# FFN layer one: inner sums in place over a column pair, and the weight difference T1 made during layer one's first half

## The chip, the cores and the metric

The kernel runs on one core of a Trainium2 chip. The metric is the device time of one execution in microseconds. TensorE (PE) multiplies 128-row tiles into PSUM, VectorE (DVE) and ScalarE (ACT) work on tiles in SBUF and PSUM, GpSimd (POOL) does little here, and SyncE (SP) issues nearly all DMAs from one queue, in order. Each engine executes its own instructions in the order in which they were written out for it; they wait for each other through semaphores.

## The reference

One decoder block over 2048 tokens of width 1024, in float32. The part before the FFN (a combined input projection, a pooling mixer, a stick-breaking attention, an output projection) is not touched by the change. The FFN that follows is:

```python
hn2 = rmsnorm(h, norm2_g)
up = jnp.einsum('bsd,df->bsf', hn2, w_up)        # 1024 -> 4096
act = jnp.square(jax.nn.relu(up))
h = h + jnp.einsum('bsf,fd->bsd', act, w_down)   # 4096 -> 1024
return rmsnorm(h, final_g)
```

## The kernel before, in words

**Arithmetic.** Each float32 operand is split into two rounded parts, hi and lo (`split`: ScalarE copies hi at L146, VectorE subtracts to get lo at L147), and each product is three matmuls: hi by hi, hi by lo, lo by hi. Both FFN layers use a scheme with seven block products instead of eight for a 2 x 2 block product (Winograd's form). It needs sums and differences of the blocks of both operands. For the activations these are called A11, A12, A22, S1, S2, S3, S4; the products are P1 to P7.

**Layer one** (`up`, matmuls at L1054). The 2048 tokens make two pairs of 512-token blocks, `q` = 0 and 1, done one after the other; these are layer one's two halves. In each, 16 columns `m` of the hidden dimension are walked in the order 0, 8, 1, 9, and so on (list `cols`): m and m + 8 are the two columns of a pair. A column has seven slots of 12 matmuls, in the order P2, P6, P5, P7, P1 of the next column, P4, P3. After each slot `post` takes what is finished out of PSUM: after P6 and P7 copies `u2`, `u3` of a bank that then goes on being summed into (L987), after P2, P7, P4 and P3 an activation block (relu L981, square L982), and the sums for layer two (L1014 to L1027), stored to DRAM tensors `sd` (L976). All these temporaries come from one pool of 13 buffers of 128 x 512 (`avp`). Weights for a slot are loaded (`rb`, L905, 1 MB a column), summed (L909 to L912) and split (`hw`) four slots ahead of their matmuls. During the first half the second pair's own sums are made too, in the columns m = 2 to 5 (`sums_second`, L940 to L946).

**Inner sums.** Three of layer two's seven products (P4, P5, P2, with the operands A22, S1, A12) are themselves done by seven inner products. Their activations need sums over the column pair and both token pairs. Before the change, in the second half, `inner_sums` does nothing at the first column of a pair but keep the block. At the second column (m from 8 on) two row blocks of the first token pair, loaded by `inner_rows` (L870) after P1, P2 and P7, meet the two blocks of the second; four VectorE operations (L881, L883, L885, L887) make four sums, two of them in fresh buffers `j1`, `j2`, and each is stored to `sdi` (L879).

**Layer two** (`down`, matmuls at L1392 for whole products, L1221 for inner ones). The order is P1, P6, P7 (eight steps each), then P4, P5, P2 (28 inner steps each), then P3. A step of P1, P6 or P7 takes one block of weights (512 KB, `wr`) and two blocks of rows (`ar`, 512 KB each), splits them into `wd` and `ad`, and runs 48 matmuls. `make_ahead` keeps up to three steps made ahead; the first one is issued at high priority, during layer one's end.

**Weight sums of layer two.** T1 = B12 - B11 and T2 = B21 - (B22 - T1) are differences of blocks of `w_down`. Before the change `more_weights`, called in every step of P1, loads B12, subtracts the step's B11 (L1115), stores T1 to DRAM (`td`, L1122) and makes four inner differences of each pair of T1 blocks, in place (`inner_weights`, L1106, stored to `wi` at L1107). In P6 the step reads T1 back, makes T2, stores it, and makes T2's inner differences; in P7 it loads B21 and makes those of B21. A step's weight work is queued in a list `late`; before the change it is taken from the list right after the step has issued its splits (for the first step, right after that step).

**Order.** Instructions are placed on each engine by a planner that simulates the program: an instruction with a lower place in the program goes first among those that are ready in the simulation, and a buffer of a pool is given to whoever is ready for it when it becomes free. `issue_after(x)` makes what follows on x's engine stand behind x. Layer two's buffers reuse layer one's memory.

Of the kernel before, what the change touches and what calls it, by code (L numbers as in the profile page):

```python
# [15 lines left out]
P = 128  # L16
# [30 lines left out]
def hymba_block(ctx: ExitStack, tc: tile.TileContext, xT, gains, w_in, pool_w, w_out, w_up, w_down, out):  # L47
# [95 lines left out]
    def split(dst, src):  # L143

        hi, lo = dst
        nc.scalar.activation(hi, src, AF.Copy)  # L146
        return nc.vector.tensor_tensor(lo, src, hi.bitcast(F32), ALU.subtract)  # L147

    later = []
    marks, gates = {}, []  # L150
# [707 lines left out]
    def up(pools, more):  # L858
# [6 lines left out]
        def inner_rows(m, i):  # L865

            halves[i, 0] = r = [avp.tile([P, T], F32, tag="av", name="hr") for _ in range(2)]
            for x in range(2):
                at = m + x * (NM // 2)
                nc.sync.dma_start(r[x], sd[0][i][at // 2][:, at % 2])  # L870

        def inner_sums(m, i, t):

            if m < NM // 2:
                halves[i, 1] = t
                return
            a, r = halves.pop((i, 1)), halves.pop((i, 0))
            m -= NM // 2
            keep = lambda n, v: nc.sync.dma_start(sdi[i][n][m // 2][:, m % 2], v)  # L879
            s1, s2 = (avp.tile([P, T], F32, tag="av", name=n) for n in ("j1", "j2"))  # L880
            nc.vector.tensor_tensor(s1, a, t, ALU.add)  # L881
            keep(0, s1)
            nc.vector.tensor_tensor(s2, s1, r[0], ALU.subtract)  # L883
            keep(1, s2)
            nc.vector.tensor_tensor(r[0], r[0], a, ALU.subtract)  # L885
            keep(2, r[0])
            nc.vector.tensor_tensor(r[1], r[1], s2, ALU.subtract)  # L887
            keep(3, r[1])

        what = {"P1": (A11, (0, 0), "Y", True, False), "P2": (A12, (0, 1), "X", True, True),  # L890
                "P6": (S2, (1, 1), "Y", False, False), "P5": (S1, (1, 0), "Z", True, False),
# [44 lines left out]
        def sums_second(n, part):  # L936
# [26 lines left out]
            else:  # L963
# [2 lines left out]
                add(s4, a12, second["s2"], ALU.subtract)  # L966
                keep(S4, s4)

        def post(q, m, s):
            k = keep.setdefault((q, m), {})  # L970
            x, y, z = (ps.get((q, m, b)) for b in "XYZ")
            new = lambda name: avp.tile([P, T], F32, tag="av", name=name)

            def put(i, t):
                if q == 0 or m >= NM // 2 or i not in (A12, A22, S1):
                    nc.sync.dma_start(sd[q][i][m // 2][:, m % 2], t)  # L976
                if q and i in (A12, A22, S1):
                    inner_sums(m, i, t)

            def act_of(i, src, t):  # L980
                nc.scalar.activation(t, src, AF.Relu)  # L981
                nc.scalar.activation(t, t, AF.Square)  # L982
                k[i] = t

            def copy(name):
                k[name] = pup.tile([P, T], F32, tag=name, name=name)
                nc.scalar.activation(k[name], y, AF.Copy)  # L987

            if s == "P1":
                copy("p1")  # L990
                if q and m >= NM // 2:
                    inner_rows(m - NM // 2, A22)
            elif s == "P2":
                if q and m >= NM // 2:
                    inner_rows(m - NM // 2, A12)
                t = new("a11")
                nc.vector.tensor_tensor(t, x, k["p1"], ALU.add)
                act_of(A11, t, t)
                put(A11, t)
            elif s == "P6":  # L1000
                copy("u2")
            elif s == "P7":
                if q and m >= NM // 2:
                    inner_rows(m - NM // 2, S1)
                copy("u3")
                t = new("a22")
                nc.vector.tensor_tensor(t, z, k["u3"], ALU.add)  # L1007
                act_of(A22, t, t)
                put(A22, t)
            elif s == "P4":  # L1010
                t = new("a21")
                act_of("A21", y, t)
                k[S1] = new("s1")
                nc.vector.tensor_tensor(k[S1], t, k[A22], ALU.add)  # L1014
                put(S1, k[S1])
                k[S2] = new("s2")
                nc.vector.tensor_tensor(k[S2], k[S1], k[A11], ALU.subtract)
                put(S2, k[S2])
                nc.vector.tensor_tensor(t, k[A11], t, ALU.subtract)
                put(S3, t)  # L1020
            elif s == "P3":
                t = new("a12")
                nc.vector.tensor_tensor(t, z, k["u2"], ALU.add)
# [14 lines left out]
        yield  # L1038
        rbb, pup, avp, psu = more()
        load(*cols[1])  # L1040
        lefts = [(g, q, s) for g, (q, m, s) in enumerate(slots) if m == 0 and not (q == 0 and s in order[:LB])]
        for g, (q, m, s) in enumerate(slots):
            while lefts and lefts[0][0] <= g + LA:
                make_left(*lefts.pop(0)[1:])
            if q == 0 and 2 <= m < 6 and s in SUMS:
                sums_second(m - 2, SUMS.index(s))
            bank, first, last = what[s][2:]
            if first:
                ps[q, m, bank] = psu.tile([P, T], F32, tag=bank, name="p" + bank)
# [20 lines left out]
    def down(pools):  # L1070
# [11 lines left out]
        steps += [("P3", S4, kk, (q,)) for q in range(2) for kk in range(8)]  # L1082
        made = {}

        def half(t, y):
            return t.rearrange("p (y c) n -> p y c n", y=2)[:, y]
# [66 lines left out]
        def make(g):  # L1153
# [12 lines left out]
                w = blk(b22, kk)  # L1166
            rows = {q: rs.tile([P, 2, T], F32, tag="ar", name="ar") for q in qs_}
            for q in qs_:
                nc.sync.dma_start(rows[q], sd[q][i][kk])
            t = t8.tile([P, 2, 4, 256], F32R, tag="wd", name="wd", align_bytes=256)  # L1170
            split((t[:, 0], t[:, 1]), w)
            left_ = {}
            for q in qs_:
                left_[q] = s8.tile([P, 2, 2, T], F32R, tag="ad", name="ad", align_bytes=256)
                split((left_[q][:, 0], left_[q][:, 1]), rows[q])
# [176 lines left out]
            while behind:  # L1352
                behind.pop(0)()

        free, held, ahead, late = 4, [], [0, 0, 0], []

        def block(t, x, c, n):
            return t[:, x, 2 * (n // 2) + c, n % 2 * P:(n % 2 + 1) * P]
# [218 lines left out]
```

## Time and profile before

| what | value |
|---|---|
| median of 3 runs | 1939.05 us (1937.96 to 1940.3) |
| the profiled execution's own time | 1938.46 us |
| its span, first to last instruction | 1936.7 us |
| granted TensorE clock, mean | 0.989 |
| busy share: PE, DVE, ACT, POOL | 98%, 74%, 52%, 9% |
| layer one's matmuls | 695.7 to some 1315 us |
| layer two's matmuls | from 1321.7 us on |

A row of the list of instructions in order of time gives start, length, engine, line, operation, output and inputs; what is in brackets at its end is the idle time of that engine ahead of it, and what ended it. A row of waits gives who waited for whom, the total in us, the number of times and the longest. A row of stretches gives the stretch, its length, the busy time (and count) of PE, PEld, DVE, ACT and POOL, the granted clock, the busy share of the DMA engines and GB/s. A store or load is "landed" when its completion is seen.

### The profile page before, as it was taken

What the parts mean: (1) busy time and instruction counts of PE and PEld (TensorE: products, weight loads), DVE (VectorE), ACT (ScalarE), POOL (GpSimd) and SP (SyncE); (2) the same over time, 40 slices, a digit from 0 to 9 for tenths busy, and PEclk for the clock granted to TensorE, in tenths of its full rate; (3) what the DMA queues carried; (4) which work ended last, traced back from release to release, by engine and by line L of the source; (5) the groups of instructions that cost most, each with busy time, mean ns of one, the idle gap of its engine ahead of it and who ended that gap; (6) DMA issues with size and microseconds to landing.
All of it is one profiled execution on the core that took longest, in us unless ns stands there. A gap on an engine that the chain in (4) does not pass through costs nothing.

```text
span 1936.7 us, 26464 instructions
## 1 busy us (share of the span) xinstructions
PE 1895.5 (98%) x8995; PEld 1581.6 (82%) x8995; DVE 1425.2 (74%) x2120; ACT 1008.5 (52%) x1598; POOL 177.2 (9%) x399
## 2 busy tenths in 40 slices
PE   9999999999999999999999999996999999999997
PEld 7888888888888888888878888875888888888886
DVE  6887799668876975767588777876566637888874
ACT  5565566455544555555575555553232345656543
POOL 0211123101211120000000000000010010020120
PEclk9999999999999999999999999997999999999999
DMA  6686686888796854577567676779899959899852
GB/s 215 205 269 189 211 285 211 268 304 271 259 356 253 314 196 168 202 245 234 195 239 265 232 261 235 278 264 394 309 326 374 341 176 309 289 299 337 300 207 90
DMA packets 200563, 502.35 MB, mean 259 GB/s; under 512 B 23648, under 2 KB 29792, under 8 KB 196320
## 3 DMA queue, kind: packets, MB, share of 16 engines
q1 hardware_dynamic: 195664, 491.89, 73.0%
q0 software_dynamic: 4608, 8.39, 2.4%
q8 instruction: 73, 1.20, 0.2%
q14 instruction: 74, 0.61, 0.1%
q10 hardware_dynamic: 144, 0.26, 0.0%
HBM read 329.53 MB, written 170.92 MB: 258 GB/s over the span
## 4 chain that ended last, share of the span: by engine, by line
PE 92%; DVE 3%; DMA 3%; issue 1%; ACT 1%; POOL 0%; SPq 0%; DVEq 0%; ACTq 0%; POOLq 0%
PE pb L1392 17%; PE pY L1054 17%; PE pb L1221 12%; PE pd L175 8%; PE pd L176 8%; PE pd L177 8%; PE pZ L1054 8%; PE pX L1054 4%; PE po L672 2%; PE pta L661 1%; DMA wr<-in_w_down_dram 1%; PE pm L202 1%; PE pz L614 1%; PE pz L615 1%; PE pr L228 1%
## 5 line engine op out<-in xcount | busy, mean ns | idle before, releaser
L1054 PE MATMUL pY<-sa,hw 128*128 128x512 f32 x1536 | 367.0, 390 | 4.4 <-ACT u L987 4.4
L1392 PE MATMUL pb<-ad,wd 128*128 128x512 f32 x1488 | 343.9, 393 | 16.2 <-ACT ad L146 16.2
L1392 PEld LDWEIGHTS pb<-ad,wd 128*128 128x128 f32 x1488 | 281.1, 189 | 75.5 <-ACT ad L146 17.3
L1054 PEld LDWEIGHTS pY<-sa,hw 128*128 128x128 f32 x1536 | 289.1, 188 | 65.3 <-ACT u L987 5.2
L175 PE MATMUL pd<-h,hl 128*128 128x512 f32 x752 | 299.6, 398 | 0.7 <-DVE qkr L421 0.7
L176 PE MATMUL pd<-h,hl 128*128 128x512 f32 x752 | 296.8, 395 | 0.0
L177 PE MATMUL pd<-h,hl 128*128 128x512 f32 x752 | 296.8, 395 | 0.0
L1221 PE MATMUL pb<-ad,wd 128*128 128x512 f32 x1008 | 228.9, 389 | 0.2 <-DVE ad L147 0.2
L1221 PEld LDWEIGHTS pb<-ad,wd 128*128 128x128 f32 x1008 | 189.2, 188 | 39.8 <-DVE ad L147 0.6
L146 ACT ACTIVATE ad<-ar 128x1024 fp32r<-128x1024 f32 x148 | 155.5, 1052 | 117.4 <-PE pb L1392 49.4
L147 DVE TENSOR_TENSOR ad<-ar,ad 128x1024 fp32r<-128x1024 f32 x148 | 179.6, 1221 | 43.5 <-ACT ad L146 43.5
L1054 PE MATMUL pZ<-sa,hw 128*128 128x512 f32 x768 | 185.9, 389 | 0.4 <-DVE a L1007 0.4
L1054 PEld LDWEIGHTS pZ<-sa,hw 128*128 128x128 f32 x768 | 144.0, 188 | 30.8 <-DVE a L1007 1.0
L175 PEld LDWEIGHTS pd<-h,hl 128*128 128x128 f32 x752 | 142.1, 189 | 28.2 <-DVE qkr L421 1.0
L177 PEld LDWEIGHTS pd<-h,hl 128*128 128x128 f32 x752 | 141.7, 188 | 27.9
L176 PEld LDWEIGHTS pd<-h,hl 128*128 128x128 f32 x752 | 142.0, 189 | 27.0
L146 ACT ACTIVATE hl<-raw 128x512 fp32r<-128x512 f32 x168 | 104.0, 630 | 111.6 <-PE pd L177 66.3
L147 DVE TENSOR_TENSOR hl<-raw,hl 128x512 fp32r<-128x512 f32 x168 | 114.2, 686 | 51.7 <-ACT hl L146 51.1
L147 DVE TENSOR_TENSOR hw<-rt,hw 128x512 fp32r<-128x512 f32 x128 | 87.2, 686 | 68.6 <-ACT hw L146 68.6
L146 ACT ACTIVATE wd<-wr 128x1024 fp32r<-128x1024 f32 x40 | 42.4, 1061 | 130.0 <-PE pb L1392 106.1
L146 ACT ACTIVATE hw<-rt 128x512 fp32r<-128x512 f32 x128 | 80.0, 626 | 28.0 <-PE pZ L1054 19.5
L1054 PE MATMUL pX<-sa,hw 128*128 128x512 f32 x384 | 93.1, 389 | 0.0
(216 smaller groups left out, 2632.0 us busy)
## 6 DMA issues: line engine op xcount, KB each, us to landing
ar<-sd SPq DMA_DIRECT2D x100, 512.0 KB, 5.6
wr<-in_w_down_dram SPq DMA_DIRECT2D x72, 512.0 KB, 6.0
rb<-in_w_up_dram SPq DMA_DIRECT2D x32, 1024.0 KB, 6.0
sd<-a SPq DMA_DIRECT2D x112, 256.0 KB, 3.7
raw<-in_w_in_dram SPq DMA_DIRECT2D x50, 512.0 KB, 4.4
ar<-sdi SPq DMA_DIRECT2D x48, 512.0 KB, 5.7
sd<-s SPq DMA_DIRECT2D x88, 256.0 KB, 4.6
raw<-in_w_out_dram SPq DMA_DIRECT2D x32, 512.0 KB, 5.7
```

The source lines that it names most:

```text
L146: nc.scalar.activation(hi, src, AF.Copy)
L147: return nc.vector.tensor_tensor(lo, src, hi.bitcast(F32), ALU.subtract)
L175: nc.tensor.matmul(ps, hl[:, 0, c], hi, start=(k == 0), stop=False)
L176: nc.tensor.matmul(ps, hl[:, 0, c], lo, start=False, stop=False)
L177: mm = nc.tensor.matmul(ps, hl[:, 1, c], hi, start=False, stop=(k == n - 1))
L202: marks["pm"] = nc.tensor.matmul(pm[:, c:c + 1], ss[:, c * P:(c + 1) * P], inv[n], start=(i == 0), stop=(i == len(parts) - 1))
L228: mm = nc.tensor.matmul(pr[:, b * P:(b + 1) * P], yr[:, x, b:b + 1].to_broadcast([P, P]), identr, start=(b == 0 and x == 0), stop=(b == TB ...
L614: nc.tensor.matmul(pz, qa[:, qsl], k, start=first, stop=False, skip_group_check=not (first and last))
L672: nc.tensor.matmul(po[:, p * 256 + to:p * 256 + to + hi - lo], vw[:, 2 * p + v], at[:, x, lo:hi], start=(p == 0 and n == 0 and x == 0), sk ...
L1054: nc.tensor.matmul(t, w[:, wx, c], a[:, ax, c % 2], start=first and c == 0 and x == 0, stop=last and c == G - 1 and x == 2, skip_group_che ...
L1221: nc.tensor.matmul(b, t[:, wx, 2 * (kk % 2) + c, i * P:(i + 1) * P], a[:, ax, c], start=p in ("P1", "P5", "P2") and kk == 0 and c == 0 and ...
L1392: nc.tensor.matmul(ps[q, n], block(t, wx, c, n), left_[q][:, ax, c], start=(n_ in ("P1", "P3") and kk == 0 and c == 0 and x == 0), stop=(n ...
```

## The change

It has three parts. First, the inner sums: each column of a pair now loads one row block (`inner_row`). At the first column the difference of row and block is made in the row's buffer and stored; at the second column the other three sums are made in the buffers that are held already. The rows are loaded after P1 for A22, after P2 for S1 and after P7 for A12. Second, `weights_first`, a generator advanced ahead of the slots P2, P5 and P4 in the columns m = 8 and on of layer one's first half, makes T1 and T1's inner differences by halves of a block (256 KB) in `avp` buffers. Third, in layer two P1's weight work is now that of B21, P6 makes and stores T2 whole, and P7 reads T2 back for its inner differences; in P1 the weight work runs up to three steps behind, and is issued behind the last row load (on SP) and the last split (on VectorE).

```diff
+        def inner_row(m, i):
+
+            halves[i, "row"] = r = avp.tile([P, T], F32, tag="av", name="hr")
+            nc.sync.dma_start(r, sd[0][i][m // 2][:, m % 2])
 
         def inner_sums(m, i, t):
 
+            r, at = halves.pop((i, "row")), m % (NM // 2)
+            keep = lambda n, v: nc.sync.dma_start(sdi[i][n][at // 2][:, at % 2], v)
             if m < NM // 2:
-                halves[i, 1] = t
+                nc.vector.tensor_tensor(r, r, t, ALU.subtract)
+                keep(2, r)
+                halves[i] = t, r
                 return
-            a, r = halves.pop((i, 1)), halves.pop((i, 0))
...
-            nc.vector.tensor_tensor(s1, a, t, ALU.add)
-            keep(0, s1)
-            nc.vector.tensor_tensor(s2, s1, r[0], ALU.subtract)
-            keep(1, s2)
-            nc.vector.tensor_tensor(r[0], r[0], a, ALU.subtract)
-            keep(2, r[0])
-            nc.vector.tensor_tensor(r[1], r[1], s2, ALU.subtract)
-            keep(3, r[1])
+            a, d = halves.pop(i)
+            nc.vector.tensor_tensor(a, a, t, ALU.add)
+            keep(0, a)
+            nc.vector.tensor_tensor(d, t, d, ALU.subtract)
+            keep(1, d)
+            nc.vector.tensor_tensor(r, r, d, ALU.subtract)
+            keep(3, r)
...
+        def weights_first():
+
+            for k in range(4):
+                b = {}
+                for x, y in ((0, 0), (0, 1), (1, 1), (1, 0)):
+                    b[x, y], t = (avp.tile([P, 2, 256], F32, tag="av", name=n) for n in ("t1", "b11"))
+                    nc.sync.dma_start(t, half(w_down[0, k + 4 * x], y))
+                    nc.sync.dma_start(b[x, y], half(w_down[1, k + 4 * x], y))
+                    yield
+                    nc.vector.tensor_tensor(b[x, y], b[x, y], t, ALU.subtract)
+                    nc.sync.dma_start(half(td[0][k + 4 * x], y), b[x, y])
+                    for to, one, two, p in {(0, 1): (((0, 0), (0, 1), (0, 0), "P5"),),
+                                            (1, 1): (((0, 1), (1, 1), (0, 1), "P7"), ((1, 1), (1, 1), (0, 0), "P6")),
+                                            (1, 0): (((1, 0), (1, 0), (1, 1), "P4"),)}.get((x, y), ()):
+                        nc.vector.tensor_tensor(b[to], b[one], b[two], ALU.subtract)
+                        nc.sync.dma_start(wi[S1][p][k // 2][:, 2 * (k % 2):2 * (k % 2) + 2], b[to])
...
             if q == 0 and 2 <= m < 6 and s in SUMS:
                 sums_second(m - 2, SUMS.index(s))
+            if q == 0 and m >= NM // 2 and s in SUMS:
+                next(first_weights, None)
...
             if n == "P1":
-                minus(blk(1, kk), w)
-                nc.sync.dma_start(td[0][kk], w)
-                inner_weights(S1, kk, w)
+                inner_weights(A12, kk, blk(2, kk))
             elif n == "P6":
                 minus(blk(2, kk, rtx), w)
-                if kk < 4:
-                    nc.sync.dma_start(half(td[1][kk], 0), half(w, 0))
-                else:
-                    nc.sync.dma_start(td[1][kk], w)
-                inner_weights(A22, kk, w)
+                nc.sync.dma_start(td[1][kk], w)
             elif n == "P7":
-                inner_weights(A12, kk, blk(2, kk))
+                inner_weights(A22, kk, blk("t2", kk))
...
+                last[0] = nc.sync.dma_start(rows[q], sd[q][i][kk])
...
+                last[1] = split((left_[q][:, 0], left_[q][:, 1]), rows[q])
+            while late and n != "P1":
+                late.pop(0)()
             late.append(lambda: more_weights(n, kk, w))
-            if g:
-                late.pop()()
...
-        late.pop()()
         make_ahead()
...
             make_ahead()
+            while len(late) > (3 if n_ == "P1" else 0):
+                with tc.issue_after(last[0].ins), tc.issue_after(last[1].ins):
+                    late.pop(0)()
```

More of the change, by code (lines that the diff above doesn't have):

```diff
@@ L147, in split, with half @@
         return nc.vector.tensor_tensor(lo, src, hi.bitcast(F32), ALU.subtract)
+    def half(t, y):
+        return t.rearrange("p (y c) n -> p y c n", y=2)[:, y]
     later = []
@@ L990, in post @@
                 copy("p1")
-                if q and m >= NM // 2:
-                    inner_rows(m - NM // 2, A22)
+                if q:
+                    inner_row(m, A22)
             elif s == "P2":
-                if q and m >= NM // 2:
-                    inner_rows(m - NM // 2, A12)
+                if q:
+                    inner_row(m, S1)
                 t = new("a11")
@@ L1002, in post @@
             elif s == "P7":
-                if q and m >= NM // 2:
-                    inner_rows(m - NM // 2, S1)
+                if q:
+                    inner_row(m, A12)
                 copy("u3")
@@ L1040, in up @@
         load(*cols[1])
+        first_weights = weights_first()
         lefts = [(g, q, s) for g, (q, m, s) in enumerate(slots) if m == 0 and not (q == 0 and s in order[:LB])]
@@ L1083, in down @@
         made = {}
-        def half(t, y):
-            return t.rearrange("p (y c) n -> p y c n", y=2)[:, y]
         def quarter(of, kp, x, y):
@@ L1168, in make @@
             for q in qs_:
-                nc.sync.dma_start(rows[q], sd[q][i][kk])
+                last[0] = nc.sync.dma_start(rows[q], sd[q][i][kk])
             t = t8.tile([P, 2, 4, 256], F32R, tag="wd", name="wd", align_bytes=256)
@@ L1174, in make @@
                 left_[q] = s8.tile([P, 2, 2, T], F32R, tag="ad", name="ad", align_bytes=256)
-                split((left_[q][:, 0], left_[q][:, 1]), rows[q])
+                last[1] = split((left_[q][:, 0], left_[q][:, 1]), rows[q])
+            while late and n != "P1":
+                late.pop(0)()
             late.append(lambda: more_weights(n, kk, w))
-            if g:
-                late.pop()()
             made[g] = t, left_
@@ L1353, in last_steps @@
                 behind.pop(0)()
-        free, held, ahead, late = 4, [], [0, 0, 0], []
+        free, held, ahead, late, last = 4, [], [0, 0, 0], [], [None, None]
         def block(t, x, c, n):
```

8 lines of the change are left out of this document (removed).

## The prediction

> **What bounds the kernel now.** I read the head of the page first, then where the 40 slices dip, then that dip by stretches, by engine in order of time, and by waits.
>
> ```profile
> span 1936.7 us, 26464 instructions
> PE 1895.5 (98%) x8995; PEld 1581.6 (82%) x8995; DVE 1425.2 (74%) x2120; ACT 1008.5 (52%) x1598; POOL 177.2 (9%) x399
> PE   9999999999999999999999999996999999999997
> PEclk9999999999999999999999999997999999999999
> ```
>
> TensorE is busy 98% of the span. A change that leaves its matmuls as they are can only win where it waits or runs at a lower clock. There is one such place before the end, slice 28, some 1307 to 1356 us: the handover from layer one of the FFN (matmuls of L1054) to layer two (L1392). Stretches around it (columns: sum of the stretch, then busy us and count of PE, PEld, DVE, ACT, POOL, the granted clock, the DMA share, GB/s):
>
> ```profile
> 715.00:945.00 230.00, 230.00 (x1020) 190.68 (x1019) 155.77 (x249) 124.00 (x219) 0.69 (x4) 1.00 0.61 208
> 1276.00:1302.00 26.00, 26.00 (x116) 21.55 (x115) 20.32 (x32) 14.36 (x25) 0.00 (x0) 1.00 0.73 247
> 1302.00:1340.00 38.00, 18.40 (x56) 13.14 (x55) 26.25 (x33) 12.13 (x16) 0.00 (x0) 0.69 1.04 402
> 1340.00:1600.00 260.00, 260.00 (x1149) 215.34 (x1148) 147.22 (x147) 90.75 (x105) 14.11 (x16) 1.00 0.89 309
> 1600.00:1765.00 165.00, 165.00 (x730) 136.67 (x729) 134.19 (x140) 94.16 (x98) 14.21 (x16) 1.00 0.94 300
> ```
>
> Only the third row has a hole. A matmul takes 0.227 us at full clock (230 us / 1020 gives 0.2255, and the chain of waits has 12 in 2.72 us). The 56 matmuls of the third row are worth 12.7 us and took 38, so the handover loses 25.3 us. TensorE's waits in that stretch (total, times, longest):
>
> ```profile
> PE pb L1392 <- ACT ad L146: 16.2, 2, 9.8
> PE pY L1054 <- ACT u L987: 3.1, 1, 3.1
> PE pZ L1054 <- DVE a L1007: 0.4, 1, 0.4
> ```
>
> The piece of the chain of waits with twelve matmuls, and TensorE's work in order of time at the handover (start, length, and in brackets the idle time ahead and what ended it):
>
> ```profile
> 1249.87 2.72 PE pX L1054 x12
> ```
> ```profile
> 1307.35 4.62 PE L1054 MATMUL pY<-sa,hw 128*128 128x512 f32 x12 [3.08 <-ACT u L987]
> 1312.33 3.02 PE L1054 MATMUL pZ<-sa,hw 128*128 128x512 f32 x12 [0.36 <-DVE a L1007]
> 1321.69 2.07 PE L1392 MATMUL pb<-ad,wd 128*128 128x512 f32 x4 [6.34 <-ACT ad L146]
> 1333.58 11.72 PE L1392 MATMUL pb<-ad,wd 128*128 128x512 f32 x39 [9.82 <-ACT ad L146]
> ```
>
> Waits make 19.7 us of the 25.3; the other 5.6 are slow matmuls, at a clock of 0.69 in the mean. Layer one's last matmul is over at 1315.35, and steady work starts at 1333.58, when VectorE has made the low half of the first activations (`ad`, L147). VectorE's order shows what stood before that:
>
> ```profile
> 1314.73 1.23 DVE L1115 TENSOR_TENSOR wr<-wr 128x1024 f32<-128x1024 f32 x1 [0.40 <-DMA wr<-in_w_down_dram]
> 1317.92 0.69 DVE L883 TENSOR_TENSOR j<-j,hr 128x512 f32<-128x512 f32 x1 [1.96 <-DMA sd<-s]
> 1319.86 1.41 DVE L1106 TENSOR_TENSOR wr<-wr 128x512 f32<-128x512 f32 x2
> 1323.65 1.42 DVE L1106 TENSOR_TENSOR wr<-wr 128x512 f32<-128x512 f32 x2 [2.39 <-DMA td<-wr]
> 1326.17 0.69 DVE L1014 TENSOR_TENSOR s<-a,a 128x512 f32<-128x512 f32 x1 [1.10 <-DMA sdi<-j]
> 1331.76 0.69 DVE L1023 TENSOR_TENSOR a<-pZ,u 128x512 f32<-128x512 f32 x1
> 1332.36 2.43 DVE L147 TENSOR_TENSOR ad<-ar,ad 128x1024 fp32r<-128x1024 f32 x2
> ```
>
> L1115 and L1106 are the weight difference T1 and its inner differences. They wait for a load and for T1's own store, and layer one's last sums (L1014 to L1023) queue behind them, then the splits. L1023 needs only products that were there at 1315.35 and runs 16.4 us later. The chain of waits goes the same way, with 7.62 us of store into L1106.
>
> ```profile
> 1315.94 7.62 DMA td<-wr
> 1323.65 0.70 DVE wr L1106
> ```
>
> ScalarE shows two lesser waits, one behind a weight load and one for a buffer, with the loads of rows that the first two steps of layer two need issued long before:
>
> ```profile
> 1305.75 1.06 ACT L146 ACTIVATE wd<-wr 128x1024 fp32r<-128x1024 f32 x1 [4.15 <-DMA wr<-in_w_down_dram]
> 1306.72 0.58 ACT L987 ACTIVATE u<-pY 128x512 f32<-128x512 f32 x1
> 1319.43 0.60 ACT L981 ACTIVATE a<-pY 128x512 f32<-128x512 f32 x1 [5.83 <-DVE hr L885]
> 1320.06 0.63 ACT L982 ACTIVATE a<-a 128x512 f32<-128x512 f32 x1
> ```
> ```profile
> 1287.32 0.95 SPq L1169 DMA_DIRECT2D ar<-sd  x2
> 1298.87 0.94 SPq L1169 DMA_DIRECT2D ar<-sd  x2
> ```
>
> **Part 1: T1 leaves the handover.** In layer two's P1 the change drops, over eight steps, 8 subtractions L1115 (1.23 us, 9.8 in all), 8 stores of T1 of 512 KB and 16 inner stores of 256 KB. P7's set of inner differences moves up in their place (8 loads, 16 subtractions L1106, 16 stores), P6's set moves to P7 and reads T2 back, and P6 stores 4 more halves of 256 KB. All told layer two loses 8 subtractions of 1.23 and 16 of 0.7 us, 21 us of VectorE, and 7.3 MB of DMA. From 1340 to 1765 that buys nothing, as TensorE never waits there; nor does the read-back of T2 cost, eight steps of 48 x 0.227 = 10.9 us after its store. The gain is the first steps: what is left of P1's weight work is now issued after the last row load and split of the steps made so far, and runs some three steps behind. No weight work stands ahead of L1014 to L1023 and the splits any more. Of the stretch's 15.3 MB (402 GB/s by 38 us), three or four loads of 512 KB, three stores of T1 and five inner stores go, nearly 5 MB.
>
> **What is late next.** After P7 the copy `u3` still has to be made before P4 goes on in the same bank, with no other column between them in the last one: at least its own 0.6 us, at most the 3.1 of now if the split `wd` still sits ahead of it. I take 1.5, since fewer loads are ahead of that one. L1007's 0.4 I halve. For P3 to layer two, P4's products are ready 12 x 0.227 = 2.7 us before the last matmul; then L981 and L982 (1.2), at worst six sums and L1023 in a row on VectorE (seven, some 0.62 apart: 4.3) and the low split (1.2), with handovers 0.5: TensorE would idle 4.5 us. At best the first split is ready earlier, its rows having been asked for at 1287, and it idles 0. I take 2.5, between, as the old order had these sums ahead of the split. Slow clock: between 0 and the 5.6 of now; I take 2, for waits a fifth as long. Left over: 1.5 + 0.2 + 2.5 + 2.0 = 6.2 us, bounds 0.6 and 13.6. Saved: 25.3 - 6.2 = 19.1, bounds 11.7 and 24.7.
>
> The granted clock after a wait, by stretches of 5 us: 0.84 around the 3.1 us wait, 0.50 inside the long ones.
>
> ```profile
> 1305.00:1310.00 5.00, 2.65 (x8) 2.16 (x9) 1.65 (x3) 2.70 (x4) 0.00 (x0) 0.84 1.02 407
> 1330.00:1335.00 5.00, 1.42 (x3) 1.16 (x4) 4.79 (x7) 2.52 (x4) 0.00 (x0) 0.50 1.05 406
> ```
>
> The Trainium skill (TensorE: Matmul & The Clock Gate, Part 1: The HAM clock gate) has only two states, half rate after an idle window of about 3.4 us and full rate again after as much work. By it my two short waits would cost no clock at all, and the sum would be 2.0 us lower; the trace, with 0.84 around a 3.1 us wait, speaks for a partial cost, so I keep the 2.0.
>
> **Part 2: T1 enters layer one's first half.** Sixteen pieces over six columns with m from 8 on: 32 loads and 32 stores of 256 KB (16.8 MB) and 32 subtractions of 0.69 us, 22 us of VectorE over some 230 us. Of the first row of the stretches above VectorE is busy 155.8 of 230; it would be 178, or 77%. DMA goes from 208 to 281 GB/s, its share from 0.61 to about 0.82, below what 1340 to 1765 bears with a full TensorE. SP issues 64 more, at some 0.47 us (the pairs of L1169 above), 30 us of the 230. I cost this at nothing. The cover is four slots of weights made ahead, 4 x 12 x 0.227 = 10.9 us, and the proof of that cover is the second token pair's sums, which already run there in four columns with DMA-fed subtractions: VectorE waited ten times for their loads, 4.4 us at the longest, and TensorE waited once in the whole of layer one before the handover, 1.3 us.
>
> ```profile
> PE pY L1054 <- ACT u L987: 1.3, 1, 1.3
> ```
> ```profile
> DVE hn L946 <- DMA hn<-hs: 18.4, 10, 4.4
> ```
>
> A store of 256 KB in that half (median us to landing last):
>
> ```profile
> sd<-a SPq DMA_DIRECT2D x60, 256.0 KB, 3.7
> ```
>
> If the cover fails: twice in each of four rounds a block is overwritten right behind its own store; eight waits of a 256 KB store's 3.7 us are 29.6 us. Queued behind such a wait are the weight splits on VectorE, and on SP the store after it and then the next 1 MB of `rb`. Bounds 0 and 29.6; I take 0, by the nearer row (the sums that are hidden now).
>
> **Part 3: inner sums in place.** Four subtractions, four stores and two row loads for each pair and operand stay; one subtraction, one store and one load move to the pair's first column. Cost nothing in the second half (1276 to 1302: TensorE full, VectorE 20.3 of 26). In the last column three sums and three loads go, and temporaries `j1`, `j2` with them; the 5.83 us wait of L981 for L885's buffer should go too. That is inside the 19.1.
>
> **Sum.** Profiled execution 1938.46 us (span 1936.7), less 19.1: 1919.4. The median of the runs, 1939.05, lies 0.6 higher: 1920.0; with the bounds 1914.4 to 1927.4.
>
> **Rivals.** (a) Forecast: 0.62.
> (b) The wait is replaced by one for data. For it: DMA is full (1.04) in the stretch, and ScalarE already waits 4.15 for a weight load. Against it: 5 MB leave, and the rows of two steps are issued by 1299. If one load of its kind (8.3 us) is waited for, with the 3.1 and the 5.6 of now, 17.0 are lost and 8.3 saved: 1930.8. Chance 0.18.
>
> ```profile
> ar<-sd SPq DMA_DIRECT2D x6, 512.0 KB, 8.3
> ```
>
> (c) Slower: the eight store waits of part 2 reach TensorE. All of them make 1920.0 + 29.6 = 1949.6; it is slower than before from 19.1 / 8 = 2.4 us each on. For it: in layer two the same pattern, L1106 behind T1's store, made VectorE wait ten times, 24.4 us, and thirteen shared buffers now hold up to five weight tiles as well. Against it: the hidden 4.4 us waits. Chance 0.11.
>
> ```profile
> DVE wr L1106 <- DMA td<-wr: 24.4, 10, 5.0
> ```
>
> The Trainium skill (DMA: Bandwidth & Descriptors, Latency and other measured facts) puts a fixed cost of about 2 us on a DMA, mostly the write's receipt from HBM. By it, as an estimate, the eight waits could not fall below 16 us together, short of the 19.1; the trace's 24.4 in ten agrees with a floor of that size.
>
> (d) The planner still puts weight work or late sums ahead of the first split, so that the deferral doesn't do what it says: 1938 to 1940. Against it is the written order behind the last split. Chance 0.05.
> (e) At the border of P1 and P6 three deferred pieces come at once, and one step of 10.9 us is lost: 1930.9. The slack of VectorE from 1340 to 1600 (147 of 260 us) speaks against it. Chance 0.04.
>
> **Numbers.** A measurement tells about 0.2% (3.9 us) from no change. Faster holds (a), (b), (e) and a mild (c): 0.85; same (d): 0.04; slower (c) and a little of (d): 0.11. The range takes (a)'s lower bound and reaches (b) and (e): 1914 to 1932, leaving out (c), (d) and a little of (a).
>
> **What would show it.** Right: slice 28 full; the first `pb` of L1392 within 5 us of the last `pZ`; no L1115 and no L1106 ahead of the first `ad` splits; TensorE without waits from 715 to 945 with DMA near 280 GB/s. Wrong: waits of `pY` or `pZ` in the first half beside subtractions that wait for a store of T1, or a handover that waits on `ar` or `wr`.

## The result, and the profile after

| | before | changed |
|---|---|---|
| median | 1937.53 us (8 runs) | 1930.3 us (8 runs, 1926.71 to 1933.59) |
| profiled execution, its span | 1938.46, 1936.7 us | 1928.68, 1926.8 us |
| ratio | | 0.996, 95% interval 0.9947 to 0.9972 |

The change makes the kernel faster by 7.2 us, 0.4%. 19.1 us had been forecast. The time lies inside the range, but the gain is well under half of what was predicted.

The head of the page, and the stretches of the changed kernel (columns as above; the second row is layer one's first half with its edges, the third the handover):

```profile
span 1926.8 us, 26479 instructions
PE   9999999999999999999999999998999999999997
```
```profile
715.00:945.00 230.00, 224.25 (x989) 184.18 (x988) 166.95 (x268) 113.83 (x206) 0.00 (x0) 1.00 0.78 270
690.00:1035.00 345.00, 338.66 (x1500) 278.88 (x1499) 254.19 (x393) 190.88 (x330) 9.51 (x15) 1.00 0.74 255
1276.00:1340.00 64.00, 55.99 (x231) 45.07 (x230) 44.95 (x64) 28.94 (x45) 0.00 (x0) 0.95 0.85 317
1340.00:1600.00 260.00, 260.00 (x1149) 215.29 (x1148) 137.71 (x133) 93.39 (x107) 14.11 (x16) 1.00 0.87 298
```

The same stretches of the kernel before:

```profile
690.00:1035.00 345.00, 343.71 (x1528) 284.75 (x1527) 241.38 (x371) 196.55 (x336) 9.53 (x15) 1.00 0.61 208
1276.00:1340.00 64.00, 44.40 (x170) 34.69 (x169) 46.57 (x65) 26.49 (x41) 0.00 (x0) 0.81 0.92 339
```

At 0.2263 us a matmul (the stretch from 1035 to 1276, in which TensorE is busy throughout, has 1065 in 241 us), the loss at the handover fell from 64 - 170 x 0.2263 = 25.5 us to 64 - 231 x 0.2263 = 11.7 us, a gain of 13.8. From 690 to 1035 us 28 fewer matmuls were done in the same time, a loss of 6.3 us. The difference is 7.5 us; the medians differ by 7.2. The two spans differ by 9.9 us; the rest lies in the part before layer one, whose program is the same. Layer one's first matmul begins at 693.08 us, 2.8 us earlier than before, and over all profiles of this study it moves between 690.96 and 696.62 us. That is 5.7 us of scatter, so I read stretches and not spans.

TensorE's waits from 690 to 1010 us, and then from 1300 us on:

```profile
PE pY L1074 <- ACT u L1004: 3.2, 2, 1.9
PE pZ L1074 <- DVE a L1024: 1.9, 2, 1.7
PE pX L1074 <- DVE hw L147: 1.3, 2, 0.7
```
```profile
PE pb L1402 <- ACT ad L146: 3.8, 1, 3.8
PE pZ L1074 <- DVE a L1024: 3.5, 1, 3.5
PE pY L1074 <- ACT u L1004: 0.7, 1, 0.7
```

VectorE at the handover, in order of time, and one row of ScalarE:

```profile
1311.66 1.23 DVE L147 TENSOR_TENSOR wd<-wr,wd 128x1024 fp32r<-128x1024 f32 x1 [3.68 <-ACT wd L146]
1314.51 0.69 DVE L1024 TENSOR_TENSOR a<-pZ,u 128x512 f32<-128x512 f32 x1 [1.62 <-DMA sd<-s]
1317.28 0.69 DVE L883 TENSOR_TENSOR a<-a,a 128x512 f32<-128x512 f32 x1 [2.08 <-ACT a L999]
...
1322.71 0.68 DVE L1040 TENSOR_TENSOR a<-pZ,u 128x512 f32<-128x512 f32 x1
1323.31 2.43 DVE L147 TENSOR_TENSOR ad<-ar,ad 128x1024 fp32r<-128x1024 f32 x2
```
```profile
1315.10 0.60 ACT L998 ACTIVATE a<-pY 128x512 f32<-128x512 f32 x1 [3.47 <-DMA sd<-a]
```

The weight work is gone from this place, as planned. What stands ahead of the first low split now is a run of ten sums of the last column (1317.28 to 1323.31). Ahead of that both blocks of the last column came late. For a22 (L1024) VectorE first did a `wd` split, for which it had idled 3.68 us, and then waited 1.62 us for a buffer that was still being stored. For a21 ScalarE's relu (L998) waited 3.47 us for a buffer. In the first half VectorE has a new wait, on the loads of T1's pieces (L978). The store waits of L983, which the prediction had priced, hardly occur:

```profile
DVE t L978 <- DMA t<-in_w_down_dram: 25.5, 9, 5.4
DVE hn L946 <- DMA hn<-hs: 17.8, 8, 4.3
DVE t L983 <- DMA td<-t: 1.2, 2, 1.0
```

### The profile page after: what moved, and what is told of

It is laid out like the page before. It is cut to its first block, busy times and chain, and to the rows that moved or that the text cites. A ratio compares the mean times of both kernels' runs of the same rounds, so it can differ in the third digit from the quotient of the medians.

```text
span 1926.8 us, 26479 instructions
## 1 busy us (share of the span) xinstructions
PE 1893.8 (98%) x8995; PEld 1579.1 (82%) x8995; DVE 1422.7 (74%) x2128; ACT 1004.0 (52%) x1598; POOL 180.6 (9%) x399
## 4 chain that ended last, share of the span: by engine, by line
PE 46%; DMA 4%; DVE 2%; issue 1%; ACT 1%; POOL 0%; SPq 0%; ACTq 0%; DVEq 0%
PE pb L1402 17%; PE pY L1074 10%; PE pb L1232 10%; PE pZ L1074 5%; PE pX L1074 3%; DMA ar<-sd 1%; DMA sd<-a 1%; DMA ar<-sdi 1%; PE pb L1345 1%; DMA su<-hn 1%; DMA sdi<-a 0%; DMA hn<-hs 0%; DMA sd<-s 0%; DMA b<-in_w_down_dram 0%; DMA t<-in_w_down_dram 0%
## 5 line engine op out<-in xcount | busy, mean ns | idle before, releaser
L998 ACT ACTIVATE a<-a 128x512 f32<-128x512 f32 x96 | 59.2, 629 | 109.3 <-DVE a L1040 54.8
```

## The experiments

Each diff is against the kernel named. Losses are worked out as above.

**Which part earns it.** Three kernels take the change apart. `inplace_only` is the kernel before with the new `inner_row` and `inner_sums` and nothing else:

```diff
-                if q and m >= NM // 2:
-                    inner_rows(m - NM // 2, A22)
+                if q:
+                    inner_row(m, A22)
...
-            s1, s2 = (avp.tile([P, T], F32, tag="av", name=n) for n in ("j1", "j2"))
+            nc.vector.tensor_tensor(a, a, t, ALU.add)
```

> The kernel before with part 3 alone: inner sums in place over both columns of a pair, T1's work where it was and not deferred. If the in-place sums by themselves free the handover: its loss falls from 25.3 to under 20 us and the time to 1932. If T1's work on VectorE holds it, as the trace of before says: loss 22 to 26 us, time 1934 to 1938.

Its median was 1929.01 us, ratio 0.9962 (0.9948 to 0.9977), as fast as the whole change. The handover, by stretch and VectorE's order:

```profile
1276.00:1340.00 64.00, 49.78 (x207) 39.41 (x206) 46.86 (x62) 27.02 (x40) 0.00 (x0) 0.92 1.00 380
```
```profile
1312.65 0.69 DVE L1103 TENSOR_TENSOR wr<-wr 128x512 f32<-128x512 f32 x1
1313.86 2.14 DVE L1103 TENSOR_TENSOR wr<-wr 128x512 f32<-128x512 f32 x3
1316.91 0.69 DVE L1103 TENSOR_TENSOR wr<-wr 128x512 f32<-128x512 f32 x1 [0.91 <-DMA td<-wr]
1320.10 2.43 DVE L147 TENSOR_TENSOR ad<-ar,ad 128x1024 fp32r<-128x1024 f32 x2
```

The loss is 17.2 us, 8.3 less than before, and the time goes down 8 us: the first expectation holds, with a larger gain than it named. T1's inner differences (L1103 here) still stand ahead of the split. But they take about 5 us, from 1312.65 to 1317.6, and VectorE waits there only 0.91 and 1.20 us for stores, where the sums and differences before were spread from 1317.9 to 1331.8. My reading is that the last column needs fewer row loads and buffers at that point; it was not tried apart.

`defer_only` is the kernel before with only the deferral:

```diff
-                minus(blk(1, kk), w)
+                w = minus(blk(1, kk), blk(0, kk))
...
-            if g:
-                late.pop()()
...
-        late.pop()()
         make_ahead()
...
+            while len(late) > (3 if n_ == "P1" else 0):
+                with tc.issue_after(last[0].ins), tc.issue_after(last[1].ins):
+                    late.pop(0)()
```

> The kernel before with the deferral of layer two's weight work alone (B11 loaded a second time in P1; inner sums as before, T1 in layer two). If the deferral is what the handover gained: the loss from 1302 to 1340 falls from 25.3 to 12 to 16 us, no waits in the first half, time 1926 to 1930. If the inner sums in place or T1's absence were needed for it: loss over 20 us, time 1933 to 1938.

```profile
1276.00:1340.00 64.00, 54.01 (x214) 42.84 (x214) 44.71 (x62) 29.54 (x44) 0.00 (x0) 0.89 0.86 309
1340.00:1600.00 260.00, 250.89 (x1096) 207.35 (x1095) 148.70 (x147) 87.20 (x100) 13.32 (x16) 0.98 0.95 330
```
```profile
1432.37 165.97 PE L1391 MATMUL pb<-ad,wd 128*128 128x512 f32 x720 [9.11 <-ACT wd L146]
```

1938.64 us, ratio 1.0007 (0.9998 to 1.0017): nothing gained. The handover lost 15.6 us, 9.9 less, as the first expectation has it; the time that it named, 1926 to 1930, did not follow. For 53 matmuls are missing in the next stretch, 12.0 us. At the border of P1 and P6 TensorE waits 9.1 us for the split of P6's first weights. VectorE makes these weights right behind the inner differences of a deferred T1 block, and those wait for that block's store, which landed 15.9 us after it was issued.

`t1_two` is the changed kernel with T1 made in P1 again, deferred:

```diff
             if n == "P1":
-                inner_weights(A12, kk, blk(2, kk))
+                w = minus(blk(1, kk), blk(0, kk))
+                nc.sync.dma_start(td[0][kk], w)
+                inner_weights(S1, kk, w)
...
-            if q == 0 and m >= NM // 2 and s in SUMS:
-                next(first_weights, None)
```

> The changed kernel with part 2 undone: T1 and its inner differences are made in layer two's P1 again, but deferred as in the change (the step's B11 is loaded a second time for it, 8 loads of 512 KB more). Theory A (layer one's first half pays 6.5 us for making T1 there): TensorE waits less than 1.5 us in the first half, the handover stays as in the changed kernel (some 11.7 us lost from 1302 to 1340), time about 6 us under the changed kernel, some 1924. Rival B (the first half's waits are chance or come from the inner sums): the waits stay and the time is 1930; rival C (the late T1 work in P1 costs again at the handover or at P6): handover 20 us or more, time 1935 or above.

```profile
1276.00:1340.00 64.00, 58.03 (x241) 46.46 (x240) 42.34 (x55) 28.67 (x41) 0.00 (x0) 0.95 0.98 360
1340.00:1600.00 260.00, 248.94 (x1091) 205.76 (x1090) 151.15 (x151) 89.58 (x103) 14.02 (x16) 0.98 0.94 321
```
```profile
PE pb L1406 <- ACT wd L146: 11.1, 1, 11.1
ACT wd L146 <- DVE wr L1130: 26.5, 6, 8.9
DVE wr L1121 <- DMA td<-wr: 13.4, 4, 5.0
```

1932.44 us, ratio 0.9979. The first half has one wait of 0.3 us left, so the 6.3 us there are part 2's. The handover loses 9.5, so the deferral and the sums in place together earn 16.0 us there. At the border the 11.1 us wait comes, with 58 matmuls (13.1 us) missing to 1600; the time lies between those of theory A and of rival C. The deferral needs T1 to be made earlier. That is what part 2 is good for, and the prediction had put no price on leaving it out.

**What the first half pays for.** In the second pair's sums a column begins with two loads of `hn`. Before, those went out 4.6 to 5.4 us ahead of the column's first pX matmul; in the changed kernel between 3.8 us ahead of it and 1.5 behind. Column m = 4, first before and then changed (SP's issues, TensorE, VectorE; L997 before is L1014 now):

```profile
862.75 0.91 SPq L945 DMA_DIRECT2D hn<-hs  x2
867.32 2.88 PE L1054 MATMUL pX<-sa,hw 128*128 128x512 f32 x12
867.49 1.42 DVE L946 SCALAR_TENSOR_TENSOR hn<-hn,gains,rlast 128x512 f32<-128x512 f32 x2 [4.05 <-DMA hn<-hs]
870.02 0.69 DVE L997 TENSOR_TENSOR a<-pX,p 128x512 f32<-128x512 f32 x1
```
```profile
866.48 0.61 PE L1074 MATMUL pX<-sa,hw 128*128 128x512 f32 x2
868.02 1.33 SPq L945 DMA_DIRECT2D hn<-hs  x2
874.09 0.75 DVE L946 SCALAR_TENSOR_TENSOR hn<-hn,gains,rlast 128x512 f32<-128x512 f32 x1 [3.38 <-DMA hn<-hs]
877.23 0.68 DVE L1014 TENSOR_TENSOR a<-pX,p 128x512 f32<-128x512 f32 x1
879.78 3.02 PE L1074 MATMUL pY<-sa,hw 128*128 128x512 f32 x12 [1.26 <-ACT u L1004]
```

VectorE's wait for them is no longer than it was, but it ends 7.6 us behind the column's first matmul instead of 0.2, so the sum out of pX (L1014) begins 10.7 us after the column's first matmul instead of 2.7. ScalarE's relu of it and the copy `u` behind that are late too. What put the loads late can be read on SP. Its queue holds the stores of T1's inner differences (L983) ahead of them, and these could only go out when VectorE had done its work behind its own waits for T1's loads. SP waited for L983 twelve times in the first half, 2.8 us of it between 863 and 868 us:

```profile
SPq L984 <- DVE t L983: 11.8, 12, 2.0
```

Four experiments on this.

`no_loads` takes away the loads that T1's first differences wait for; T1 is then the difference of two other tiles:

```diff
-                    nc.sync.dma_start(t, half(w_down[0, k + 4 * x], y))
-                    nc.sync.dma_start(b[x, y], half(w_down[1, k + 4 * x], y))
                     yield
-                    nc.vector.tensor_tensor(b[x, y], b[x, y], t, ALU.subtract)
+                    nc.vector.tensor_tensor(b[x, y].rearrange("p c n -> p (c n)"), rlast[:, 0], sslast, ALU.subtract)
```

> The changed kernel without the 32 loads of 256 KB that T1's pieces in layer one wait for: each first difference is taken of two tiles that lie in memory already (T1 is then not the weights' difference; all subtractions and stores are there). Theory L (VectorE's waits for these loads, 25.5 us in nine, push the posts, the next weight load and the second pair's loads late, so two waits fall together): the loads of the second pair's sums go out again 4 to 5 us ahead of their column's first pX matmul, first-half waits of TensorE under 1.5 us, time some 1924. Theory V (the 32 added subtractions or the stores do it): waits of 4 us or more stay, time 1929 to 1931.

1921.23 us, ratio 0.9924. The stretch from 690 to 1035 has 1520 matmuls (1528 before, 1500 changed), so 4.5 of the 6.3 us are back; two waits of 1.7 and 1.2 us are left, which is more than the 1.5 expected. The `hn` loads lead pX by some 1 to 5 us. The added subtractions and stores are all there, so theory V falls. But with the loads 8.4 MB of transfers and each piece's second buffer go as well, so this run alone doesn't part the wait for the loads from these. The handover also lost less in this run (8.8 us for 11.7), of which I had expected nothing.

`early_hn` is the changed kernel with those `hn` loads issued three slots earlier:

```diff
+            if q == 0 and 9 <= m < 13 and s == "P4":
+                sums_second(m - 9, -1)
```

> The changed kernel with one thing moved: the first two loads of the second pair's sums in each of their four columns are issued three slots (8 us) earlier, in T1's column ahead. Nothing is left out and VectorE does the same work. If the first half's waits come of these loads going out only when the column's pX matmuls begin: waits of TensorE from 690 to 1035 under 2.5 us (6.5 in the changed kernel), time some 1924 to 1926. If VectorE is simply late by T1's own waits: waits of 4 us or more stay, time 1929 to 1931.

```profile
690.00:1035.00 345.00, 342.04 (x1513) 282.75 (x1512) 256.89 (x396) 193.77 (x332) 10.02 (x15) 1.00 0.75 258
1276.00:1340.00 64.00, 56.13 (x232) 45.16 (x231) 45.18 (x64) 29.16 (x45) 0.00 (x0) 0.95 0.86 318
```
```profile
PE pY L1084 <- ACT u L1012: 2.1, 1, 2.1
PE pX L1084 <- DVE hw L147: 0.8, 1, 0.8
```

1925.41 us, ratio 0.9938. Its handover is that of the changed kernel (232 matmuls for 231), so this is the cleanest comparison: 13 matmuls, 2.9 us, come back, and waits are 2.9 us in place of 6.4 (2.5 had been the limit set). The late `hn` loads are about half of part 2's price. The rest I put down to T1's own load waits (L978's counterpart still 18.7 us here); that was not tried apart.

`late_cols` puts T1's pieces into the last five columns of the first half, `split_cols` into columns 1 to 3 and 11 to 13 of the order, both off the columns of the second pair's sums:

```diff
-            if q == 0 and m >= NM // 2 and s in SUMS:
+            if q == 0 and n_col(q, m) > 10 and s in SUMS + ("P7",):
                 next(first_weights, None)
```
```diff
+            if 1 <= n_col(q, m) <= 3 and s in SUMS or 11 <= n_col(q, m) <= 13 and s in SUMS + ("P7",):
                 next(first_weights, None)
```

> T1 is made in layer one's first half still, but in the last five columns, behind those in which the second pair's sums are made. Theory A1 (the waits come from both tasks sharing the 13 buffers, so the sums' loads go out later): no waits of pY and pZ over 0.5 us in the columns m = 3, 4, 5, all together under 2 us in the first half, time some 1925. Rival A2 (VectorE's added load and its waits for the weight loads do it, wherever they stand): 4 to 7 us of waits, now in the last five columns, time 1929 to 1932.

> T1 in layer one's first half, but in columns 1 to 3 and 11 to 13 of the order, three or four pieces each, so that neither the second pair's sums (columns 4 to 10) nor the turn to the second pair (columns 14, 15) meets it. If only the meeting of the two tasks costs: waits under 1 us from 690 to 1035 (2.6 in the run with the last five columns), time 1917 to 1921. If the pieces cost by themselves: waits of 3 us or more, 1923 to 1927.

`late_cols`: 1920.74 us, ratio 0.9922 (0.9908 to 0.9936); one wait of 0.2 us up to 1010, but three, 2.4 us together, at the turn to the second pair (1015 to 1031). `split_cols`: 1921.17 us, ratio 0.9917 (0.9904 to 0.993); 1.5 us of waits from 690 to 1040, somewhat more than the 1 us expected, and 1525 matmuls from 690 to 1035. In `split_cols` VectorE still waited 16.6 us for T1's loads, in eight waits, and almost none of it reached TensorE. So the place matters, as theory A1 says: it is the meeting of two tasks that each wait for DMA in VectorE's order which costs, not either alone. The cause that A1 names, the 13 shared buffers, is another question; `av15` below is on that. Both lose 8 to 9 us at the handover, less than the changed kernel; neither shows the pZ wait of 3.5 us there.

**Buffers.** `av15` gives the shared pool 15 buffers (SR, the loads of the activation sums, goes from 3 to 2 to make room); `late_av15` joins that with `late_cols`; `split_hl5` joins `split_cols` with 15 buffers taken from the split weights.

```diff
-SR = 3
+SR = 2
...
-..., spool("rbb", 1), spool("avp", 13)
+..., spool("rbb", 1), spool("avp", 15)
```

> The changed kernel with 15 buffers in the shared pool in place of 13 (the buffers for the loads of layer one's activation sums go from 3 to 2 to make room). If buffers hold up the sums' loads and, at the handover, the last column's blocks a22 and a21 (1.62 us and 3.47 us behind a store): first-half waits under 3 us, the pZ wait of 3.5 us at the handover falls under 1.5, time 1921 to 1926. If buffers are not the cause: waits as in the changed kernel, 1929 to 1932.

```profile
1276.00:1340.00 64.00, 60.63 (x260) 49.45 (x259) 48.16 (x69) 34.45 (x53) 0.00 (x0) 0.97 0.93 342
```

1925.64 us, ratio 0.9942. Half of the expectation came true: the handover loses 5.2 us, with no pZ wait, and neither a22 nor a21 waits for a buffer there. But the first half still waits 6.0 us, with the `hn` loads as late as in the changed kernel, and has 1484 matmuls for 1500, which takes back 3.6 us. So the shared buffers hold up the handover in the changed kernel, and are not what makes the first half wait; the load buffer that was given up may be what costs there.

> T1 in the last five columns of the first half together with 15 buffers in the shared pool. If the two gains (6 us in the first half, some 6 at the handover) are of different causes they add, less the crowding at the turn to the second pair: loss from 1302 to 1340 of 4 to 6 us, time 1916 to 1919. If they are the same gain: 1920 to 1922.

1928.81 us, slower than both expectations: the gains don't add. With two load buffers the turn to the second pair waits 7.4 us (1002 to 1042), mostly for the splits of the activation sums, the longest 3.5 us.

> T1 in columns 1 to 3 and 11 to 13 with 15 buffers in the shared pool, the room taken from the split weights (5 buffers in place of 6) and not from the activation loads. If the buffers' gain at the handover adds: loss from 1302 to 1340 some 5 us (8.1 without), waits at the turn to the second pair under 1.5 us, time 1916 to 1919. If five split-weight buffers are too few: waits of pX, pY, pZ on hw, over 3 us in layer one, time 1922 or more.

1923.28 us, ratio 0.9928. Its handover lost 64 - 246 x 0.2263 = 8.3 us, no less than the 8.1 of `split_cols`, with 2.4 us of waiting for the copy `u`, and the first half has 1510 matmuls for 1525. With another buffer taken away the two added ones didn't help.

**The rest of the handover.** `no_inner_last` leaves out the inner sums of layer one's very last column:

```diff
             a, d = halves.pop(i)
+            if m == NM - 1:
+                keep(0, a)
+                keep(1, d)
+                keep(3, t)
+                return
```

> The changed kernel without the inner sums of layer one's very last column: three row loads and nine VectorE operations are left out there, the nine stores stay (of other data). If the handover's rest is VectorE's queue (ten sums ahead of the first low split) and the buffers that the last column waits for: the loss from 1302 to 1340 falls from 11.7 to 4 to 7 us, time 1923 to 1926. If it is the DMA's fullness: the loss stays over 9 us, time 1928 to 1931.

```profile
1276.00:1340.00 64.00, 61.58 (x262) 49.87 (x261) 40.29 (x55) 30.41 (x46) 0.00 (x0) 0.97 0.90 335
```

1919.83 us, ratio 0.9907. The loss is 4.7 us, 7.0 less, with the DMA as full as before (1.04 from 1302 to 1340). The last column's sums, with their three row loads and their buffers, are most of what is left of the handover, and a full DMA by itself is not. So the last experiment keeps all the work, and queues six of those sums behind the first low split (on top of `split_cols`; `sums` are the three operations of S1 and of A12 in the last column):

```diff
+            if m == NM - 1 and i != A22:
+                tail_sums.extend(sums)
...
+                while tail_sums:
+                    tc.add_manual_dep(tail_sums.pop().ins, last[1].ins.name,
+                                      mybir.DependencyInfo(mybir.DependencyClass.NoSync, mybir.DependencyReason.DATA),
+                                      reason="behind the first split")
```

> T1 in columns 1 to 3 and 11 to 13, and in addition the last column's inner sums of S1 and A12 (six VectorE operations) are queued behind the first low split of layer two. If VectorE's queue is what the handover still waits for (5.1 us on the first split): that wait falls under 2 us, the loss from 1302 to 1340 from 8.1 to 4 or 5 us, time 1917 to 1919. If the split waits for rows or for its buffer: wait over 4 us, time as with the columns alone, 1920 to 1922.

```profile
690.00:1035.00 345.00, 344.10 (x1529) 284.57 (x1528) 262.22 (x406) 197.10 (x338) 10.01 (x15) 1.00 0.75 259
1276.00:1340.00 64.00, 59.85 (x255) 48.19 (x254) 41.78 (x56) 29.99 (x44) 0.00 (x0) 0.97 0.96 355
```
```profile
1303.77 3.01 PE L1079 MATMUL pZ<-sa,hw 128*128 128x512 f32 x12
1306.95 1.20 PE L1411 MATMUL pb<-ad,wd 128*128 128x512 f32 x4 [0.17 <-ACT ad L146]
1311.43 33.86 PE L1411 MATMUL pb<-ad,wd 128*128 128x512 f32 x142 [3.28 <-ACT ad L146]
```

1916.87 us, ratio 0.9897 (0.9883 to 0.9911): the fastest of all, 20 us under the kernel before and some 12 under the changed one (by the two ratios, 0.9897 and 0.996). The loss is 6.3 us, not the 4 or 5 expected. The wait on the split fell from 5.1 to 3.3 us and not to under 2: seven operations, where there were ten, still stand ahead of it.

## Why the prediction was wrong

- **What bounds the kernel** was right: 25.5 us lost at the handover, and what took VectorE's work out of the way there shortened it, by 8.3 us (the sums in place), 9.9 (the deferral) and 16.0 (both).
- **"I cost this at nothing"** (part 2) is the step that failed first. It cost 6.3 us. The cover was taken from the second pair's sums, whose waits of 4.4 us are hidden when they come alone. That T1's pieces wait for their own loads too, and push those sums' loads later in SP's queue, was not in it. The bound of 29.6 us was put on the wrong transfer: on T1's stores (1.2 us of waits measured) and not on its loads (25.5 us). It counted two overwrites a round behind their own store; a third follows one subtraction later. Rival (c) had the right queue and the wrong transfer.
- **"Left over: 6.2 us"** at the handover is the other mis-sized term: 11.7 us were left, inside the bounds of 0.6 and 13.6 but near their end. The wait of P3 on L1007's successor, taken at 0.2, was 3.5 us: that sum came behind a `wd` split, for which VectorE idled 3.68 us, and then behind a buffer, 1.62 us. The low split, taken at 2.5, waited 3.8, behind ten operations and not seven. The statement that the buffer wait "should go too" was wrong: the block a21 (L998) still waited 3.47 us for a store. The forecast gain of 19.1 less these two errors, 5.5 at the handover and 6.3 in the first half, is 7.3; 7.2 was measured. That they meet so well is partly luck, given the 5.7 us of scatter ahead of layer one.
- **"Inside the 19.1"** (part 3): by itself it earns 8 us, as much as the whole change. I had put nearly all of the gain on the deferral.
- **Rival (e)**, at 0.04, is real wherever T1 stays in P1: waits of 9.1 and 11.1 us. In the change it doesn't come up, because part 2 moves T1 away. TensorE kept its 1149 matmuls from 1340 to 1600.
- **What layer two saves bought nothing**, as said.
- **The clock**: slow matmuls at the handover come to 11.7 - 8.0 = 3.7 us with waits of 0.7, 3.5 and 3.8 us, against the 2.0 taken. Two stretches of the changed kernel show them, behind the two longer waits:

```profile
1315.00:1320.00 5.00, 4.75 (x14) 3.76 (x15) 2.92 (x6) 3.10 (x5) 0.00 (x0) 0.66 0.87 336
1325.00:1330.00 5.00, 5.00 (x17) 3.95 (x16) 4.75 (x5) 3.37 (x5) 0.00 (x0) 0.66 0.73 249
```

  The Trainium skill (TensorE: Matmul & The Clock Gate, Part 1: The HAM clock gate) has half rate after an idle window of about 3.4 us, for about as long. For two waits just over that it gives, as an estimate, 2 x 3.4 / 2 = 3.4 us, and the 3.7 here agree with it.

  The length of the wait does not decide it in these runs, though. Twelve matmuls took 4.62 us behind the 3.08 us wait of the kernel before, 4.62 behind one of 2.35 in `split_hl5` and 4.61 behind one of 2.15 in `early_hn`, about as long as behind the 3.54 us here (4.59); behind 2.54 us in `inplace_only` they took 3.01. So the 0.84 that the prediction read as a partial cost was a whole one, in a stretch that was half idle, and why some shorter waits cost it and others don't is open.
- **What was to show it**: the weight work is gone from ahead of the first `ad` splits, and the first `pb` follows the last `pZ` at once; but slice 28 has 8 tenths, the steady matmuls begin 4.8 us later, and TensorE did wait from 715 to 945, with `pY` and `pZ` beside the sums of the second pair. Of the signs of being wrong, the handover's wait for weights came in part: the split ahead of a22 waited 1.40 us on ScalarE for a load of `wr`.
- **DMA in the first half** was 270 GB/s from 715 to 945, at a share of 0.78 (forecast 281 and 0.82). That term was right, and was not the limit.

What stays open: why the changed kernel and `early_hn` have the pZ wait of 3.5 us at the handover, and `late_cols`, `split_cols` and `no_loads`, with as many buffers and the same code there, have not. The traces show the step at which they part. In the first two the last column's two rows (`hr`) are asked for as the last pY matmuls begin (1308.67 us, and 1308.71 and 1308.93), in the three others 4.1 to 4.6 us ahead of them. a22 waits for its buffer in all five (1.4 to 1.9 us), but the last `wd` split ahead of it makes VectorE idle in the first two alone (3.68 and 3.46 us), and a21 waits for a buffer in those two alone (3.47 and 3.44 us). What makes SP late there stays unknown.

## What to carry to other kernels

A wait that is hidden today is no proof that a second one beside it will be: add up the waits that follow one another in one engine's order, and ask which loads the first one makes late. When an engine's work is deferred past a handover, look for its reader: the deferral alone gave back 12 us at the next border. And before crediting a change of several parts to its largest, run the smallest alone.

## What the runs showed that was not expected

Placing the same 32 loads, 32 subtractions and 32 stores in other columns of the same half moved the time by 8 to 9 us (1930.3 to 1921.2; ratios 0.996 and 0.9917); 25 matmuls (5.7 us) of it lie in that half, and the handover lost 3.6 us less. 16.6 us of VectorE's waits for loads cost TensorE 1.5 us there, and 25.5 us of them, in columns next to the other DMA-fed task, cost 6.3. The part of the program that no kernel here touched varied by 5.7 us between profiles, nearly as much as the gain that was found. And matmuls at half the clock, for over 3 us, followed a wait of 2.15 us (`early_hn`) as well as those of 3.5.
